# Mixing-layer weights of the first stream: high parts by casting DMA, low parts by an accumulating DMA, loads two units ahead

## The chip, the cores and the metric

The kernel runs on one core of one Trainium2 chip. The metric is device time in microseconds (us). Before the change the median of three runs is 2050.35 us (2050.03 to 2053.55). One profiled execution of the same kernel took 2050.04 us; all rows below come from it.

Engines have short names in the rows: PE is TensorE (PEld its weight loads), DVE is VectorE, ACT is ScalarE, POOL is GpSimd, SP is SyncE. An engine's name with a q behind it (SPq, POOLq) is its instruction queue where it issues a DMA or waits.

## What is computed

One encoder layer on two streams of 512 tokens with 1024 features (a prompt and a sample), each on its own:

```
x = x + 0.5 * swiglu(rms_norm(x, ffn1_norm), ffn1_w_gate, ffn1_w_up, ffn1_w_down)
h = rms_norm(x, mix_norm)
proj = h @ w_in            # q k v | mlstm q k v | 16 gates | o_pre | g_att | g_mlstm
att = gqa_block_attention(rope(rms_norm(aq)), rope(rms_norm(ak)), av)   # 8 heads of 64, 2 kv heads
mem = mlstm_bidirectional(mq, mk, mv, gate_pre, ..., o_pre, ...)        # 4 heads of 128, both directions
merged = sigmoid(g_att) * (att @ w_up_att) + sigmoid(g_mlstm) * (mem @ w_up_mlstm)
x = x + merged @ w_out
x = x + 0.5 * swiglu(rms_norm(x, ffn2_norm), ffn2_w_gate, ffn2_w_up, ffn2_w_down)
```

All inputs and weights are float32 in HBM. Both streams use the same weights.

## The kernel before

**Split arithmetic.** Every large product is made from float32r operands that come in two parts, a high part `hi` (the value rounded to float32r) and a low part `lo` (the value minus `hi`), as three matmuls: hi·hi, hi·lo and lo·hi. So each weight is needed as such a pair. A pair of 1024 columns on 128 partitions, `w`, holds 2 x 512 KB and serves 24 matmuls of 128x512.

**Stages.** The first feed-forward block (helpers at L372 and L630) runs first, then the mixing layer of the prompt, `mix(0)`, then that of the sample, `mix(1)`, then the second feed-forward block. In the trace the mixing layer of the prompt lies between about 640 and 1045 us. Inside it come, in this order: the projections to k, v, gates and q (`tok_proj`, L797); the first mLSTM queries and keys (`mem_qk`); the attention of 8 heads, whose chain of scores (L1083), maximum, exponential (L1088), scaling (L1091, L1093), transposes (L1099), split (L713, L714) and values (L1110) leaves gaps on PE, which are filled with projection matmuls handed out a few at a time (`among`, L817); the mLSTM values (`mem_values`, L797 again); four mLSTM heads (`mem_head`: products L1234, twenty exponentials each at L1248; `mem_out`); eight projections for the merge gate (`mem_gate`, L830) and eight for the mLSTM's way up (`merge_mem`, four weights that each serve two units), one after the other with little else between; and w_out.

**How a weight comes in.** A unit is a pair (load, compute). `go(...)` (L768) calls a unit's load and holds its compute back until the next unit's load has been called. `load_w` (L286) is that load. In `mix(0)` it calls `fetch_w`: SP fetches the raw weight from HBM into a tile `wr` (L271; four buffers). `split_w` then makes the pair in a tile `w` (tag `w8`, four buffers): ACT writes `hi` as a rounded copy (L278), DVE writes `lo` as raw minus `hi` (L279). SP then writes both parts to a scratch area in DRAM, `wpark` (L301), and `mix(1)` reads the pair back from there, with no split of its own. `shifted(-60)` gives ACT's and DVE's part an earlier place in the order.

**Order.** The engines' instruction orders are fixed when the program is built, by a scheduler that goes by these priorities; instructions inside `pin(...)` keep the order in which the code writes them. A DMA waits in its queue's order: what stands behind it on that queue waits too.

**Other names.** `box` tiles (four) hold a broadcast copy of the mLSTM gate sums, `ebuf`, for one head: SP reads them (L1053), and POOL or DVE adds a mask (L1056). The mLSTM's queries and keys of a head (`qk`) lie, for the prompt, in one buffer of tag `w8`; for the sample in two of tag `wr`. `gate_tops` (L983) makes two small transposes (L984, L985) of the gates' running maximum.

Of the kernel before, what the change touches and what calls it, by code (L numbers as in the profile page):

```python
# [9 lines left out]
F32R = mybir.dt.float32r  # L10
# [16 lines left out]
def encoder(ctx, tc, I, outs):  # L27
# [233 lines left out]
    def fetch_w(view, behind=None):  # L261

        views = view if isinstance(view, list) else [view]
        shape = list(views[0].shape)
        shape[2] = sum(v.shape[2] for v in views)
        raw = wpool.tile(shape, F32, tag="wr", bufs=4, name=nm("wr"))
        if behind is not None:
            nc.gpsimd.tensor_copy(raw[:, 0, 0:1], behind)
        c = 0
        for v in views:  # L270
            nc.sync.dma_start(raw[:, :, c:c + v.shape[2]], v)  # L271
            c += v.shape[2]
        return raw
# [9 lines left out]

    parked = {}

    def load_w(view, key):  # L286


        if key in parked:
            d, shape = parked[key]  # L290
            w2 = wpool.tile(shape, F32R, tag="w8", bufs=4, name=nm("w"))
            for i in range(2):
                nc.sync.dma_start(f(w2[:, i]), d[:, i])
            return w2[:, 0], w2[:, 1]
        raw = fetch_w(view)
        with shifted(-WEIGHTS):
            hi, lo = split_w(raw, V_)
        shape = [P, 2] + list(raw.shape[1:])
        parked[key] = d, _ = dpool.tile(shape, F32, name=nm("wpark")), shape
        for i, t in enumerate((hi, lo)):  # L300
            nc.sync.dma_start(d[:, i], f(t))  # L301
        return hi, lo


# [459 lines left out]


    held = []

    def go(*units):  # L768
        for load, comp in units:
            held.append((comp, load()))  # L770
            while len(held) > 1:
                c, w = held.pop(0)
                c(w)

# [29 lines left out]
    def proj(view, key, src, n, done):  # L804

        def comp(w):
            done(proj_w(*w, src, n))

        def steps(w):
            p = []  # L810

            def step(k, i):
                if not p:
                    p.append(MM())
                (wh, wl), (sh, sl) = w, src(k)
                a, b = ((wh, sh), (wh, sl), (wl, sh))[i]
                pin(nc.tensor.matmul(p[0], a[:, k, :], b, start=(k == 0 and i == 0), stop=(k == n - 1 and i == 2)))  # L817
                if k == n - 1 and i == 2:
                    done(p[0])
            return [lambda k=k, i=i: step(k, i) for k in range(n) for i in range(3)]  # L820

        comp.steps = steps
        return (lambda: load_w(view, key)), comp

    def proj_w(wh, wl, src, n, p=None):
        p = p or MM()
# [10 lines left out]
    def mix(s, xh, xl, early=None, extra=None, after=None):  # L837
# [143 lines left out]

        def gate_tops(run, top):
            p = PT()  # L983
            nc.tensor.transpose(p[:, 0:32], run, ident[0:32, 0:32])  # L984
            nc.tensor.transpose(p[:, 32:64], top.to_broadcast([32, P]), ident[0:32, 0:32])  # L985
            V_.tensor_copy(st[:, 0:2], p[:, 0:64].rearrange("p (i d b h) -> p i d b h", i=2, d=2, b=4))


# [12 lines left out]

        def mem_qk(h, j):
            def done(pp):
                if j == 0 and not s:
                    t = wpool.tile([P, 4, S], F32R, tag="w8", bufs=4, name=nm("qk"))
                    qks[h] = [t[:, i] for i in range(4)]
                elif s:
                    t = wpool.tile([P, 2, S], F32R, tag="wr", bufs=4, name=nm("qk"))
                    qks.setdefault(h, []).extend(t[:, i] for i in range(2))
                t = pp  # L1010
                if not s:
                    t = F2()
# [6 lines left out]
        def out_gate(h):  # L1019
# [3 lines left out]
                ogs[h] = og  # L1023
            return win_cols(2320 + h * P, done)

        def q_rope(pr):
            return rope_steps(qraw[:, :, pr * P:(pr + 1) * P], rq[0][:, :, 2 * pr:2 * pr + 2], tabs[0])

# [6 lines left out]
        go(*tok_proj(xh, xl, [(512, 256), (2304, 16)], 2, kv_done, (PS, PS, MM, MM)))  # L1035
        if early:
            early()
        go(*tok_proj(xh, xl, [(0, 512)], 2, q_done, (MM, PO, MM, MM)), mem_qk(0, 0))
        yield None
        tops = gates()  # L1040
        list(q_rope(0))
        with shifted(60):
            k_turn()
            q_turn(0, lambda i: i)
        gate_tops(*tops)
        yield None
        go(mem_qk(0, 1), mem_qk(1, 0), mem_qk(1, 1))

        def mem_rows(h, d):

# [86 lines left out]
                    between.extend(c.steps(w))  # L1137
                between.pop(0)()

        def att_gate(d):  # L1140
            def done(pp):
                gate_of(mg[:, d, :], pp)
            return win_cols(2832 + d * P, done)

        queue.extend(att_gate(d) for d in range(4))
        queue.extend(out_gate(h) for h in range(HM))
        queue.extend(att_gate(d) for d in range(4, 6))
        if not s:
# [8 lines left out]
        for h in range(HA):  # L1157
            nxt = []
            for b in range(4):
                if h in (0, 2, 4) and b == 2:  # L1160
                    q_turn(h // 2 + 1, pin)
                if (h, b) in ((0, 3), (2, 3)):
                    rope = q_rope(h // 2 + 2)
                if h < 4:
                    next(rope, None)
                if h + 1 < HA:
                    nxt.append(score(h + 1, b))
                among(FILLER[0])
# [17 lines left out]
        def up_unit(part, d, src, done, bank=None):  # L1186
            def load():
                if d % 2 == 0:
                    wv = I[("w_up_att", "w_up_mlstm")[part]][0].rearrange("(k p) c -> p k c", p=P)
                    wups[part, d // 2] = load_w(wv[:, :, d * P:(d + 2) * P], ("up", part, d))  # L1190

            def comp(_):
                wu = wups[part, d // 2]
                cl = slice((d % 2) * P, (d % 2 + 1) * P)
                done(proj_w(wu[0][:, :, cl], wu[1][:, :, cl], lambda k: (src[:, k, 0, :], src[:, k, 1, :]), 4,
                            bank and bank()))
            return load, comp
# [100 lines left out]
        for h in range(HM):  # L1298
            Ts = mem_head(h)
            if h == 0:  # L1300
                go(*mem_values())
            queue.append(merge_att(2 * h))
            fill(1)
            mem_out(h, Ts)
            if h + 2 < HM:
                queue.extend([att_gate(h + 6), mem_qk(h + 2, 0), mem_qk(h + 2, 1)])
            queue.append(merge_att(2 * h + 1))
            fill(99)

        mh, ml = A([P, KD, S], F32R, "mh"), A([P, KD, S], F32R, "ml")  # L1310
# [539 lines left out]
```

## Time and profile before

| | |
|---|---|
| median of the runs | 2050.35 us (2050.03 to 2053.55) |
| profiled execution | 2050.04 us |
| its span | 2048.3 us, 1.7 us less than that execution's time |
| PE busy | 2032.9 us, 99% |
| DVE busy | 1564.0 us, 76% |
| ACT busy | 901.6 us, 44% |
| POOL busy | 93.1 us, 5% |
| SP's DMA queue | 450.27 MB, 65.2% of the 16 DMA engines' span |

PE is granted full clock all along (0.999 on average). A group row names line, engine, operation, output<-input, shapes and count, then busy us, mean ns of one, and the idle time before it with what ended that. A DMA row names count, KB each and the median us from issue to landing.

### The profile page before, as it was taken

What the parts mean: (1) busy time and instruction counts of PE and PEld (TensorE: products, weight loads), DVE (VectorE), ACT (ScalarE), POOL (GpSimd) and SP (SyncE); (2) the same over time, 40 slices, a digit from 0 to 9 for tenths busy, and PEclk for the clock granted to TensorE, in tenths of its full rate; (3) what the DMA queues carried; (4) which work ended last, traced back from release to release, by engine and by line L of the source; (5) the groups of instructions that cost most, each with busy time, mean ns of one, the idle gap of its engine ahead of it and who ended that gap; (6) DMA issues with size and microseconds to landing.
All of it is one profiled execution on the core that took longest, in us unless ns stands there. A gap on an engine that the chain in (4) does not pass through costs nothing.

```text
span 2048.3 us, 26765 instructions
## 1 busy us (share of the span) xinstructions
PE 2032.9 (99%) x9317; PEld 1678.7 (82%) x9317; DVE 1564.0 (76%) x2772; ACT 901.6 (44%) x1647; POOL 93.1 (5%) x116
## 2 busy tenths in 40 slices
PE   9999999999999999999999999999999999999998
PEld 7888888888888878888878888888888888888887
DVE  8888888886797888786566746446788988786797
ACT  7644444442234567563324553324444444442224
POOL 0000000001003000100120000001000000000001
PEclk9999999999999999999999999999999999999999
DMA  9656566799766853868684345677655655599753
GB/s 318 199 168 224 176 201 195 243 344 351 262 224 225 289 165 126 274 227 286 202 316 157 113 141 188 217 260 253 195 185 186 198 173 185 199 344 344 273 200 119
DMA packets 311014, 457.96 MB, mean 224 GB/s; under 512 B 20232, under 2 KB 182112, under 8 KB 309600
## 3 DMA queue, kind: packets, MB, share of 16 engines
q1 hardware_dynamic: 308800, 450.27, 65.2%
q0 software_dynamic: 1920, 5.72, 0.8%
q8 instruction: 73, 1.20, 0.2%
q14 instruction: 61, 0.50, 0.1%
q10 hardware_dynamic: 160, 0.27, 0.0%
HBM read 288.25 MB, written 167.94 MB: 223 GB/s over the span
## 4 chain that ended last, share of the span: by engine, by line
PE 94%; DVE 3%; ACT 1%; DMA 1%; issue 0%; SPq 0%; ACTq 0%; DVEq 0%
PE mm L830 15%; PE pst L372 12%; PE pso L372 12%; PE mm L372 10%; PE mm L630 8%; PE pss L372 6%; PE mm L817 5%; PE pss L630 4%; PE pst L630 4%; PE mm L797 4%; PE pso L630 3%; PE pso L1110 1%; PE pss L1083 1%; PE pst L1099 1%; PE pso L1284 1%; PE pss L1234 1%
## 5 line engine op out<-in xcount | busy, mean ns | idle before, releaser
L372 PE MATMUL pst<-xc,w 128*128 128x512 f32 x1056 | 253.6, 389 | 0.0
L372 PEld LDWEIGHTS pst<-xc,w 128*128 128x128 f32 x1056 | 198.2, 188 | 41.1
L372 PE MATMUL mm<-xc,w 128*128 128x512 f32 x972 | 229.6, 390 | 0.5 <-ACT f L380 0.5
L372 PEld LDWEIGHTS mm<-xc,w 128*128 128x128 f32 x972 | 182.0, 188 | 38.4 <-ACT f L380 0.9
L630 PE MATMUL mm<-rt,w 128*128 128x512 f32 x765 | 178.7, 389 | 0.0
L830 PE MATMUL mm<-xh,w 128*128 128x512 f32 x560 | 176.2, 392 | 0.0
L630 PEld LDWEIGHTS mm<-rt,w 128*128 128x128 f32 x765 | 143.5, 188 | 29.8
L330 ACT ACTIVATE w<-t 128x512 fp32r<-128x512 f32 x176 | 106.5, 627 | 135.7 <-issue 63.1
L331 DVE TENSOR_TENSOR w<-t,w 128x512 fp32r<-128x512 f32 x176 | 117.7, 687 | 41.5 <-ACT w L330 39.9
L372 PE MATMUL pss<-xc,w 128*128 128x512 f32 x528 | 126.8, 389 | 0.0
L372 PE MATMUL pso<-xc,w 128*128 128x512 f32 x528 | 126.8, 389 | 0.0
L372 PE MATMUL pso<-xc,f 128*128 128x512 f32 x528 | 126.8, 389 | 0.0
L830 PEld LDWEIGHTS mm<-xh,w 128*128 128x128 f32 x560 | 104.9, 188 | 21.5
L372 PEld LDWEIGHTS pso<-xc,f 128*128 128x128 f32 x528 | 99.1, 188 | 20.6
L372 PEld LDWEIGHTS pss<-xc,w 128*128 128x128 f32 x528 | 99.1, 188 | 20.6
L372 PEld LDWEIGHTS pso<-xc,w 128*128 128x128 f32 x528 | 99.1, 188 | 20.6
L817 PE MATMUL mm<-xh,w 128*128 128x512 f32 x336 | 114.6, 401 | 0.0
L830 PE MATMUL mm<-xl,w 128*128 128x512 f32 x280 | 109.7, 392 | 0.0
L713 ACT ACTIVATE w<-wr 128x512 fp32r<-128x512 f32 x72 | 45.1, 632 | 137.2 <-PE pso L630 71.8
L713 ACT ACTIVATE w<-t 128x512 fp32r<-128x512 f32 x82 | 51.8, 632 | 107.4 <-PE pst L630 62.4
L630 PE MATMUL pss<-rt,w 128*128 128x512 f32 x396 | 93.7, 389 | 0.0
L630 PE MATMUL pst<-rt,w 128*128 128x512 f32 x396 | 93.7, 389 | 0.0
(440 smaller groups left out, 4005.6 us busy)
## 6 DMA issues: line engine op xcount, KB each, us to landing
rt<-rbuf SPq DMA_DIRECT2D x154, 512.0 KB, 5.4
wpark<-w SPq DMA_DIRECT2D x104, 512.0 KB, 3.5
w<-wpark SPq DMA_DIRECT2D x104, 512.0 KB, 4.9
wr<-in_ffn_w_gate_dram SPq DMA_DIRECT2D x62, 512.0 KB, 5.4
rbuf<-tab SPq DMA_DIRECT2D x102, 256.0 KB, 3.9
wr<-in_ffn_w_up_dram SPq DMA_DIRECT2D x44, 512.0 KB, 4.5
rbuf<-f SPq DMA_DIRECT2D x72, 256.0 KB, 4.1
wr<-in_w_in_dram SPq DMA_DIRECT2D x36, 512.0 KB, 6.4
```

The costliest lines, as they stand in the source:

```text
L330: pin(nc.scalar.activation(t[:, 0], src, AF.Copy))
L331: pin(V_.tensor_tensor(t[:, 1], src, f(t[:, 0]), op=ALU.subtract))
L372: nc.tensor.matmul(p, a[:, k, :], xt[:, b, k, :], start=(first and k == 0 and i == 0), stop=(k == HK_ - 1 and i == 2), skip_group_check=True)
L630: nc.tensor.matmul(p, u[:, a, d * P:(d + 1) * P], r[:, b, ts], start=(first and q == 0 and k == 0), stop=(q == len(us) - 1 and k == 2), sk ...
L713: nc.scalar.activation(hi, src, AF.Copy)
L797: nc.tensor.matmul(p[b][:, :N], a[:, k, bs], w_[:, kl, :], start=(k == 0 and i == 0), stop=(k == KD - 1 and i == 2))
L817: pin(nc.tensor.matmul(p[0], a[:, k, :], b, start=(k == 0 and i == 0), stop=(k == n - 1 and i == 2)))
L830: nc.tensor.matmul(p, a[:, k, :], b, start=(k == 0 and i == 0), stop=(k == n - 1 and i == 2))
L1083: pin(nc.tensor.matmul(p, qT[:, h, b * P:(b + 1) * P], kv[:, hk * 2 + j, :], start=(j == 0), stop=(j == 1)))
L1099: pin(nc.tensor.transpose(p[:, b * P:(b + 1) * P], Ps[b][:, kb * P:(kb + 1) * P], ident))
L1110: pin(nc.tensor.matmul(pos[h], Vst[:, kb, h // 4, :], w, start=(kb == 0 and i == 0), stop=(kb == 3 and i == 1)))
L1234: nc.tensor.matmul(p, qk[a][:, isl], qk[b], start=(n == 0), stop=(n == 2))
```

## The change

`load_w` gets a flag `cast`. It is set for the 28 units that `win_cols` makes (8 `mem_qk`, 4 `out_gate`, 8 `att_gate`, 8 `mem_gate`) and for the 8 loads of `w_up_att` and `w_up_mlstm`: 36 weights of 512 KB. For these, in `mix(0)`, POOL's queue issues a DMA from HBM straight into `hi`, which rounds to float32r on the way; ACT writes `lo = -hi`; POOL's queue issues a second DMA from HBM that adds the raw weight onto `lo`. SP's raw fetch, the `wr` tile and DVE's subtraction are gone for them; the two writes to `wpark` stay. The weights of `tok_proj` (keys, values, gates, queries, mLSTM values) and of w_out come in as before.

`go` holds two units instead of one. The two transposes of `gate_tops` are pinned behind the second score of the second attention head. `mem_qk` units and the first `att_gate` are called earlier, the prompt's `qk` tiles lie in two `wr` buffers per head as the sample's do, and `merge_att(1)` is queued beside `merge_att(0)`. This applies to both streams, except where `not s` is written; the casting path acts in `mix(0)` alone, since `mix(1)` finds its pairs parked.

```diff
-    def load_w(view, key):
+    def load_w(view, key, cast=False):
...
-        raw = fetch_w(view)
-        with shifted(-WEIGHTS):
-            hi, lo = split_w(raw, V_)
-        shape = [P, 2] + list(raw.shape[1:])
+        if cast:
+            hi, lo = cast_w(view)
+        else:
+            raw = fetch_w(view)
+            with shifted(-WEIGHTS):
+                hi, lo = split_w(raw, V_)
+        shape = [P, 2] + list(hi.shape[1:])
         parked[key] = d, _ = dpool.tile(shape, F32, name=nm("wpark")), shape
         for i, t in enumerate((hi, lo)):
             nc.sync.dma_start(d[:, i], f(t))
+        return hi, lo
+
+    def cast_w(view):
+
+        w2 = wpool.tile([P, 2] + list(view.shape[1:]), F32R, tag="w8", bufs=4, name=nm("w"))
+        hi, lo = w2[:, 0], w2[:, 1]
+        nc.gpsimd.dma_start(hi, view)
+        with shifted(-WEIGHTS):
+            nc.scalar.activation(lo, f(hi), AF.Copy, scale=-1.0)
+            nc.gpsimd.dma_start(lo, view, accum_op=ALU.add)
         return hi, lo
...
     held = []
+    AHEAD = 2
...
-            while len(held) > 1:
+            while len(held) > AHEAD:
...
-        return (lambda: load_w(view, key)), comp
+        return (lambda: load_w(view, key, key[0] == "in")), comp
...
-            nc.tensor.transpose(p[:, 0:32], run, ident[0:32, 0:32])
-            nc.tensor.transpose(p[:, 32:64], top.to_broadcast([32, P]), ident[0:32, 0:32])
+            pin(nc.tensor.transpose(p[:, 0:32], run, ident[0:32, 0:32]))
+            pin(nc.tensor.transpose(p[:, 32:64], top.to_broadcast([32, P]), ident[0:32, 0:32]))
...
-                if j == 0 and not s:
-                    t = wpool.tile([P, 4, S], F32R, tag="w8", bufs=4, name=nm("qk"))
-                    qks[h] = [t[:, i] for i in range(4)]
-                elif s:
-                    t = wpool.tile([P, 2, S], F32R, tag="wr", bufs=4, name=nm("qk"))
-                    qks.setdefault(h, []).extend(t[:, i] for i in range(2))
+                t = wpool.tile([P, 2, S], F32R, tag="wr", bufs=4, name=nm("qk"))
+                qks.setdefault(h, []).extend(t[:, i] for i in range(2))
...
-        go(*tok_proj(xh, xl, [(0, 512)], 2, q_done, (MM, PO, MM, MM)), mem_qk(0, 0))
+        go(*tok_proj(xh, xl, [(0, 512)], 2, q_done, (MM, PO, MM, MM)), mem_qk(0, 0), mem_qk(0, 1))
...
-        gate_tops(*tops)
         yield None
-        go(mem_qk(0, 1), mem_qk(1, 0), mem_qk(1, 1))
+        go(mem_qk(1, 0), mem_qk(1, 1), att_gate(0))
...
-        queue.extend(att_gate(d) for d in range(4))
+        queue.extend(att_gate(d) for d in range(1, 4))
...
+                if (h, b) == (0, 1):
+                    gate_tops(*tops)
...
-                    wups[part, d // 2] = load_w(wv[:, :, d * P:(d + 2) * P], ("up", part, d))
+                    wups[part, d // 2] = load_w(wv[:, :, d * P:(d + 2) * P], ("up", part, d), True)
...
-            fill(1)
+            if h == 0:
+                queue.append(merge_att(1))
+            fill(2)
...
-            queue.append(merge_att(2 * h + 1))
+            if h:
+                queue.append(merge_att(2 * h + 1))
```

Three places in the instruction orders show what this moves. The number at the end of a name is that of one buffer use.

**POOL in the stretch of mLSTM heads and merge gates.** Before the change POOL's whole order between the gates' copies (L952, L954) and the low parts of the merge (L714) is one row:

```order
L952 COPY Is_430_5645<-gt_363_5277 128x16
L954 COPY Is_430_5645<-gt_363_5277 128x4 x4
L1056 TENSOR_TENSOR box_360_5274<-box_360_5274,tab_301_4214 128x512 x6
L714 TENSOR_TENSOR ml_911_8043<-mg_365_5279,mh_910_8042 128x512 x6
L952 COPY Fs_1050_8991<-gt_985_8558 128x16
```

Now (L311 the casting DMA, L314 the accumulating one, same queue; the eight `mem_gate` weights begin with w_891, the four of `w_up_mlstm` with w_921):

```order
L311 DMA w_894_8031<-in_w_in_dram 128x8x128
L314 DMA w_894_8031<-in_w_in_dram 128x8x128
L311 DMA w_897_8052<-in_w_in_dram 128x8x128
L314 DMA w_897_8052<-in_w_in_dram 128x8x128
L311 DMA w_901_8087<-in_w_in_dram 128x8x128
L314 DMA w_901_8087<-in_w_in_dram 128x8x128
L311 DMA w_905_8122<-in_w_in_dram 128x8x128
L314 DMA w_905_8122<-in_w_in_dram 128x8x128
L311 DMA w_909_8157<-in_w_in_dram 128x8x128
L311 DMA w_913_8192<-in_w_in_dram 128x8x128
L314 DMA w_909_8157<-in_w_in_dram 128x8x128
L314 DMA w_913_8192<-in_w_in_dram 128x8x128
```

Each weight has two issues on one queue, and but for a few pairs the next weight's cast stands behind this weight's accumulate.

**SP around the end of the attention.** `wr` tiles here are the raw mLSTM values' weights (128x2x512), `box` the gate sums of a head. Before:

```order
L271 DMA wr_642_6651<-in_w_in_dram 128x8x128
L301 DMA wpark_568_6326<-w_567_6323 128x1024 x2
L271 DMA wr_733_7038<-in_w_in_dram 128x2x512
L301 DMA wpark_594_6432<-w_593_6429 128x1024 x2
L271 DMA wr_736_7046<-in_w_in_dram 128x2x512
L301 DMA wpark_618_6544<-w_617_6541 128x1024 x2
L271 DMA wr_743_7082<-in_w_in_dram 128x2x512
```

Now:

```order
L304 DMA wpark_586_6429<-w_585_6425 128x1024 x2
L304 DMA wpark_609_6540<-w_608_6536 128x1024 x2
L1067 DMA box_360_5274<-ebuf_367_5281 128x4x128
L271 DMA wr_721_7026<-in_w_in_dram 128x2x512
L271 DMA wr_724_7034<-in_w_in_dram 128x2x512
L1067 DMA box_360_5274<-ebuf_367_5281 128x4x128
L304 DMA wpark_723_7031<-w_722_7028 128x1024 x2
```

The first two of these fetches stood among the attention's traffic; now they stand behind a read into `box` for the second mLSTM head.

**ACT at the same place.** L1248 (now L1259) are the first mLSTM head's twenty exponentials, L1261 (now L1272) the scaling after them, L278 the high part of a raw weight. Before:

```order
L278 ACTIVATE w_737_7048<-wr_736_7046 128x1024
L1088 ACTIVATE t2_693_6860,asm_692_6858<-pss_691_6855,asm_692_6858 128x512
L713 ACTIVATE t2_695_6869<-pst_694_6864 128x512
L1088 ACTIVATE t2_699_6880,asm_698_6878<-pss_697_6875,asm_698_6878 128x512
L713 ACTIVATE t2_701_6889<-pst_700_6884 128x512
L1091 ACTIVATE t2_699_6880<-t2_699_6880,asm_698_6878 128x512
L713 ACTIVATE t2_704_6900<-pst_703_6895 128x512
L1121 ACTIVATE f2_707_6907<-pso_690_6852 64x512
L713 ACTIVATE t2_709_6915<-pst_708_6910 128x512
L713 ACTIVATE t2_713_6927<-pst_712_6922 128x512
L713 ACTIVATE t2_716_6938<-pst_715_6933 128x512
L1248 ACTIVATE t2_722_6976<-box_360_5274,st_368_5282 128x128
```

Now:

```order
L1259 ACTIVATE t2_720_7009<-box_360_5274,st_368_5282 128x128
L1272 ACTIVATE t2_710_6964<-t2_710_6964,dn_708_6959 128x128
L1272 ACTIVATE t2_713_6977<-t2_713_6977,dn_708_6959 128x256
L1272 ACTIVATE t2_716_6990<-t2_716_6990,dn_708_6959 128x384
L278 ACTIVATE w_722_7028<-wr_721_7026 128x1024
L1272 ACTIVATE t2_719_7003<-t2_719_7003,dn_708_6959 128x512
L278 ACTIVATE w_725_7036<-wr_724_7034 128x1024
```

The first two weights of the mLSTM values were split during the attention; now their split stands behind the first head's exponentials.

More of the change, by code (lines that the diff above doesn't have):

```diff
@@ L1024, in out_gate, with att_gate, done @@
             return win_cols(2320 + h * P, done)
+        def att_gate(d):
+            def done(pp):
+                gate_of(mg[:, d, :], pp)
+            return win_cols(2832 + d * P, done)
         def q_rope(pr):
@@ L1138, in among @@
                 between.pop(0)()
[L1140 to L1143, printed above, removed]
-        queue.extend(att_gate(d) for d in range(4))
+        queue.extend(att_gate(d) for d in range(1, 4))
         queue.extend(out_gate(h) for h in range(HM))
```

## The prediction

> **What bounds the kernel now.** First the head of the page, then the chain that ended last.
>
> ```profile
> span 2048.3 us, 26765 instructions
> PE 2032.9 (99%) x9317; PEld 1678.7 (82%) x9317; DVE 1564.0 (76%) x2772; ACT 901.6 (44%) x1647; POOL 93.1 (5%) x116
> PE 94%; DVE 3%; ACT 1%; DMA 1%; issue 0%; SPq 0%; ACTq 0%; DVEq 0%
> ```
>
> PE is busy for all but 15 us of the span. The change takes no matmul away, so it can gain only what PE now waits, and can lose without such a limit. The waits of PE between 640 and 1060 us, the whole mixing layer of the prompt:
>
> ```profile
> PE pst L984 <- DVE kv L931: 1.5, 1, 1.5
> PE pss L797 <- DVE t L1215: 0.8, 1, 0.8
> PE pst L1099 <- ACT t L1091: 0.7, 1, 0.7
> PE pst L1099 <- DVE t L1093: 0.4, 1, 0.4
> PE pst L1099 <- DVE t L714: 0.3, 1, 0.3
> PE pst L1099 <- DVE qT L1033: 0.3, 1, 0.3
> ```
>
> They sum to 4.0 us; none is a wait for a weight. Weights now always come in time. How much time they have shows in three stretches (columns: PE busy with its count, PEld, DVE, ACT, POOL, clock, DMA share, GB/s):
>
> ```profile
> 664.00:700.00 36.00, 35.90 (x169) 29.18 (x169) 25.77 (x55) 18.27 (x26) 0.00 (x0) 1.00 0.94 310
> 700.00:803.00 103.00, 101.15 (x500) 82.31 (x499) 90.76 (x185) 70.02 (x138) 0.00 (x0) 1.00 0.51 170
> 700.00:803.00 103.00, 66.14 (x240) 43.37 (x240) 1.00 0.51 170
> 925.00:982.00 57.00, 57.00 (x253) 46.99 (x252) 39.91 (x60) 20.20 (x30) 6.79 (x5) 1.00 0.83 279
> ```
>
> The third row is the second one for L817 alone. A weight serves 24 matmuls. In the attention 240 of L817 are 10 weights in 103 us, 10.3 us each. In the merge stretch 57.00 / 253 is 0.2253 us a matmul, so PE takes a weight in 24 x 0.2253 = 5.41 us. There a new supply path decides.
>
> **What is removed.** DVE's subtraction, 36 times, and SP's fetches:
>
> ```profile
> L279 DVE TENSOR_TENSOR w<-wr,w 128x1024 fp32r<-128x1024 f32 (+1 forms) x56 | 70.3, 1258 | 25.6 <-ACT w L278 21.3 <-DMA f<-xbuf 3.2 <-DMA wr<-in_w_in_dram 0.9
> L278 ACT ACTIVATE w<-wr 128x1024 fp32r<-128x1024 f32 x38 | 39.6, 1054 | 43.7 <-issue 18.0 <-PE mm L830 8.2 <-PE pss L1234 7.6
> ```
>
> 36 x 1.26 = 45 us of DVE go, off PE's path but for the waits listed. If all DVE- and ACT-made waits went, L984's too (its transposes are moved), that is 4.0 us. A little more may hide in the spacing of the attention's matmuls, 401 ns against 389 where nothing interrupts:
>
> ```profile
> L817 PE MATMUL mm<-xh,w 128*128 128x512 f32 x336 | 114.6, 401 | 0.0
> L630 PE MATMUL mm<-rt,w 128*128 128x512 f32 x765 | 178.7, 389 | 0.0
> ```
>
> 240 x 0.011 = 2.6 us at most. After 1060 us both kernels read parked pairs, and between 1060 and 1400 us PE's list of waits is one row, word for word the fifth above, so two units ahead gain at most 0.3. Gains lie between 0 and 6.9; I take 4, the waits that have a row. ACT's negation has the size of its old copy, 1.05 us, so ACT's work is unchanged.
>
> **What is added: a queue that takes turns.** For a weight POOL issues a cast (L311), ACT negates, POOL issues the accumulate (L314), and mostly the next cast stands behind that. While the accumulate waits for ACT, and ACT for the cast's landing, the next weight's transfer can't start; SP's fetches now have no such coupling and run a few weights ahead. Rows for the prices:
>
> ```profile
> L745 POOL DMA_DIRECT2D f<-in_c_rope_dram x1 | 0.9, 918 | 0.0
> L1324 POOL DMA_DIRECT2D x2buf<-f x16 | 8.9, 556 | 381.8 <-DVE f L1323 376.9 <-DVE cs L967 5.0
> wr<-in_w_in_dram SPq DMA_DIRECT2D x11, 512.0 KB, 4.7
> wr<-in_w_in_dram SPq DMA_DIRECT2D x6, 512.0 KB, 6.5
> wr<-in_w_up_mlstm_dram SPq DMA_DIRECT2D x4, 512.0 KB, 5.5
> w<-wpark SPq DMA_DIRECT2D x104, 512.0 KB, 4.9
> wpark<-w SPq DMA_DIRECT2D x104, 512.0 KB, 3.5
> out_dram<-t SPq DMA_DIRECT2D x8, 256.0 KB, 2.2
> GB/s 318 199 168 224 176 201 195 243 344 351 262 224 225 289 165 126 274 227 286 202 316 157 113 141 188 217 260 253 195 185 186 198 173 185 199 344 344 273 200 119
> ```
>
> Issue: L745 has 1024 runs, as a weight of 128x8x128 has, and took 0.92 us (128 runs: 0.56); I take 0.92. Landing of a cast: no casting or accumulating DMA is in the trace. A plain fetch of 512 KB landed in 4.7 us in the attention's window (700 to 830 us, first of the rows) and 5.5 to 6.5 in the merge stretch (890 to 960). Low end: the quickest 256 KB, 2.2, plus 256 KB more at 351 GB/s, 0.75: 3.0 us. High end 6.5. I take 5.2, between the quiet fetch and the up-projections' fetch. Landing of an accumulate: it must also read its target. At least as the cast; at most the quiet fetch and a full read of the tile as long as its park, 4.7 + 3.5 = 8.2. I take 5.7, near the plain fetches, since reading and writing can overlap. Behind one another on a queue: 512 KB at 351 GB/s is 1.5 us at least; I take 2.0 since the parks share the engines.
>
> One turn, from one accumulate's issue to the next: the next cast is issued 0.92 later and lands at 0.92 + 5.2 = 6.1, but not before the accumulate's data plus 2.0, 5.7 + 2.0 = 7.7; then ACT's 1.05 with 0.1 each for two semaphores. 7.7 + 1.25 = 8.95 us. This is under the attention's 10.3 us, so the attention hides it, and 3.54 us over the merge stretch's 5.41.
>
> A rule speaks against the change on top. DVE's scaling in the attention works from SBUF to SBUF:
>
> ```profile
> L1093 DVE TENSOR_SCALAR t<-t,asm 128x512 f32<-128x512 f32 x16 | 7.7, 484 | 0.3
> ```
>
> The Trainium skill, SBUF — State Buffer, its box on the "DVE blocks DMA" trap, says that while DVE runs an operation in a two-port mode, GpSimd can't write descriptors, so its DMAs start late. If L1093 is such an operation, an issue could be late by up to 0.48 us; that lies in the attention's spare 1.35 us a turn, so the sum would be the same, and no run so far shows it.
>
> The sum, place by place.
>
> *Start-up.* The first seven cast weights are used one behind the other at about PE's 36 us for 169 matmuls (7 x 24 = 168), so the seventh is needed about 37 us after the first. The queue gives five turns and one pair (two casts together, 2.0 apart): 5 x 8.95 + 2.0 = 46.8. The first is about 4.4 us early (a cast of 5.2, ACT, an accumulate of 5.7 after the gates' copies). Loss 46.8 - 37 - 4.4 = 5.
>
> *End of the attention.* Now PE fills the last head's gaps with the mLSTM values' projection:
>
> ```profile
> 812.93 0.60 ACT L713 ACTIVATE t<-pst 128x512 fp32r<-128x512 f32 x1 [0.30 <-PE pst L1099]
> 813.43 1.56 ACT L1248 ACTIVATE t<-box,st 128x128 f32<-128x128 f32 x5
> 806.83 0.43 SPq L271 DMA_DIRECT2D wr<-in_w_in_dram  x1
> 840.83 5.96 ACT L1248 ACTIVATE t<-box,st 128x128 f32<-128x128 f32 x20
> 803.00:824.90 21.90, 14.23 (x56) 10.55 (x57) 1.00 0.43 151
> ```
>
> The last row is L797 alone. After the change its first fetch stands on SP behind a read into `box`, and its `wr` buffer is freed by the first head's products; these wait for PSUM that the exponentials and DVE free, so I put the fetch at the fifteenth of twenty exponentials: 15 x 0.30 = 4.5 us after 813.4. Then 0.43 issue, 5.5 landing, 1.05 ACT, 0.1: 825. Up to there PE did 56 matmuls of L797, 56 x 0.2253 = 12.6 us, for which it now has nothing. Without them the last head's chain ends 2 to 3 us sooner. Loss 10. If the fetch gets its buffer and queue place in time, nothing: that is the other end.
>
> *Heads, 820 to 925 us.* Casts come in clumps of three weights that PE takes in 5.4 us each. POOL's queue also has mask additions (1.53 us each), and the negation can stand behind one head's exponentials, 5.96 us:
>
> ```profile
> L1056 POOL TENSOR_TENSOR box<-box,tab 128x512 f32<-128x512 f32 x6 | 9.2, 1526 | 218.4 <-DMA wpark<-w 161.2 <-DMA box<-ebuf 49.2 <-ACT mg L861 8.0
> ```
>
> One clump overruns its reserve by two turns, 2 x 3.54 = 7. Nothing if the reserve holds; 14 if two do.
>
> *Merge stretch.* Twelve weights at 5.41 us. The first is ready about 5.5 us early: its buffer is free three weights ahead, 16.2 us, of which casting, negating and accumulating take 5.2 + 1.25 + 5.7 = 12.2, with 1.5 us of slower need ahead of it. Of the eleven after it nine take a turn and two come as the second of a pair, 2.0 behind the first: 9 x 3.54 - 2 x 3.41 = 25.0, less 5.5 is 19.5. As the need of raw data doubles, the floor by bytes is 4 x 0.524 MB at 351 GB/s (cast, accumulate, two parks), 6.0 us a weight: 12 x 0.6 = 7 even with an ideal queue.
>
> Sum 5 + 10 + 7 + 19.5 = 41.5, and 37.5 with the gain of 4. 2048.3 + 37.5 + 1.7 outside the span = 2087.5, so **2087 us**; the profiled execution is 0.3 us under the median of the runs, so nothing is to be added.
>
> **Rivals.**
>
> *The queue keeps up.* If cast and accumulate land in 3.0 us and follow each other in 1.5, a turn is 3.0 + 1.5 + 1.25 = 5.75 us. The merge stretch then loses 12 x 0.34 = 4 less 5.5 in reserve, nothing; start-up and heads nothing. With the fetch of the values in time too it leaves the gain of 4.0 to 6.9 from 2050.0: 2043 to 2046, faster. For: a POOL queue that does nothing else; against: no 512 KB fetch in these windows landed under 4.7 in the median.
>
> The Trainium skill, DMA: Bandwidth & Descriptors, in its section on the anatomy of a DMA from GpSimd, fits such a DMA as 2.0 us plus its bytes over 436 GB/s; for 512 KB that is an estimate of 3.2 us, which would make this rival true. The trace's only repeated DMA from POOL speaks against it, since by that fit 256 KB would be 2.6 us:
>
> ```profile
> x2buf<-f POOLq DMA_DIRECT2D x16, 256.0 KB, 4.6
> ```
>
> *The accumulate is slow.* At 8.2 us a turn is 8.2 + 2.0 + 1.25 = 11.45, above the attention's 10.3 as well: 1.15 x 10 = 11 more there, 2.5 x 9 = 22 more in the merge stretch, 2.5 x 5 = 12 at the start, some 15 in the heads. 2087 + 60 = 2147. It decides from an accumulate of 7.0 us on (turn 10.3).
>
> *Only the attention's end counts.* Quick DMAs as in the first rival, but the late fetch: 10 less 4.0 to 6.9, 2053 to 2056.
>
> **How the numbers follow.** Forecast 0.53 (its own range 2066 to 2112); queue keeps up 0.19; only the attention's end 0.12; slow accumulate 0.16. The range 2043 to 2135 leaves out most of the slow accumulate and little else. A measurement of this kernel can tell about 0.2%, 4 us, from no change: faster needs under 2046. Faster 0.17, all but a little of the first rival; same 0.09, the rest of it and the lower half of the third; slower 0.74, the others.
>
> **What would show it.** Each step is right if PE's list of waits has L830 and L817 behind POOL's accumulate, twelve times some 3 us between 950 and 1020 us; if L314's issues on POOL lie about 9 us apart there and 10 in the attention; if casts land in 5 and accumulates in 5 to 6 us; and if PE has a gap of some 10 us before its first L811. It is wrong if POOL's issues follow PE at 5.4 us (first rival), if POOL's turns exceed 10 us already in the attention (slow accumulate), or if the gap before L811 is missing.

## The result: 2168.88 us, and the profile after

The changed kernel takes 2168.88 us in the median (2167.0 to 2171.86, 4 runs) against 2050.64 us (2050.03 to 2053.55, 4 runs): slower by a factor of 1.0574, 95% interval 1.0561 to 1.0587, some 118 us. The forecast was 2087, with a range up to 2135. The direction was right, the size a third of what came.

The head of the page of the kernel after, and the chain that ended last:

```profile
span 2167.0 us, 26814 instructions
PE 2071.4 (96%) x9317; PEld 1698.1 (78%) x9317; DVE 1526.8 (70%) x2736; ACT 901.8 (42%) x1647; POOL 177.4 (8%) x188
PE 79%; issue 8%; DMA 6%; DVE 3%; ACT 2%; POOL 2%; SPq 0%; POOLq 0%; ACTq 0%; DVEq 0%
```

PE has the same 9317 matmuls. It is idle for 95.6 us of the span instead of 15.4, and *busy* for 38.5 us longer. DVE lost 37 us of work (45 were forecast), and the kernel is slower all the same.

PE's waits in the kernel after (what waited <- what ended it: total, times, longest):

```profile
PE pss L1097 <- ACT t L1102: 11.9, 2, 9.8
PE mm L844 <- DMA w<-in_w_in_dram: 10.6, 4, 3.9
PE pss L844 <- DMA w<-in_w_up_mlstm_dram: 10.4, 2, 6.3
PE pso L1295 <- ACT t L726: 10.2, 3, 4.7
PE pss L1245 <- DVE t L1261: 7.1, 5, 2.9
```

None of these stood in the list before. Only the second and third are waits for a weight by name. The first and fourth are attention scores and mLSTM values that wait for ACT.

Where the time goes can be read by comparing both kernels at the same amount of PE's work. For each matmul I took the distance from its start to the next one's; what exceeds the distance at full clock (0.227 us for 512 columns) is lost. The lost time up to a point, less what the kernel before had lost at that point, in us:

| up to | end of first projections | middle of attention | late attention | first mLSTM head | start of merge stretch | end of merge stretch | end |
|---|---|---|---|---|---|---|---|
| after | 1 | 42 | 43 | 54 | 84 | 117 | 118 |

So the start-up and the first half of the attention cost 41 us, some 12 and some 29 (predicted: 5 and nothing), the second half nothing, the end of the attention 11 (predicted 10), the heads 30 (predicted 7), the merge stretch 33 (predicted 19.5).

How POOL's queue runs, in the first half of the attention, where POOL's casts and accumulates and SP's writes to `wpark` are the only transfers:

```profile
733.78 1.54 POOL L314 DMA_DIRECT2D w<-in_w_in_dram  x1 [7.58 <-ACT w L313]
734.66 1.68 POOL L311 DMA_DIRECT2D w<-in_w_in_dram  x1
743.72 1.55 POOL L314 DMA_DIRECT2D w<-in_w_in_dram  x1 [7.38 <-ACT w L313]
744.61 1.57 POOL L311 DMA_DIRECT2D w<-in_w_in_dram  x1
753.21 1.55 POOL L314 DMA_DIRECT2D w<-in_w_in_dram  x1 [7.03 <-ACT w L313]
754.09 1.58 POOL L311 DMA_DIRECT2D w<-in_w_in_dram  x1
```

The predicted alternation is there: accumulate (L314), next cast (L311) 0.9 us behind it, then 7 to 8 us of waiting for ACT's negation. From accumulate to accumulate it is 743.72 - 733.78 = 9.94 and 753.21 - 743.72 = 9.49 us; the five turns from 714 to 764 us took 9.5 to 10.6, 9.9 in the mean. I had put 8.95. An accumulate landed in 6.4 us (I had put 5.7), with hardly any spread for those issued from 723 to 764 us, and the cast issued behind it landed 1.7 to 2.6 us later than it (I had put 2.0).

What the prediction missed is what ACT does meanwhile (start, duration, instruction, in brackets the idle time before):

```profile
722.17 1.06 ACT L313 ACTIVATE w<-w 128x1024 fp32r<-128x1024 f32 x1 [3.90 <-DMA w<-in_w_in_dram]
723.14 0.61 ACT L726 ACTIVATE qk<-f 128x512 fp32r<-128x512 f32 x1
732.34 1.06 ACT L313 ACTIVATE w<-w 128x1024 fp32r<-128x1024 f32 x1 [8.59 <-DMA w<-in_w_in_dram]
733.30 0.61 ACT L726 ACTIVATE qk<-f 128x512 fp32r<-128x512 f32 x1
733.94 0.69 ACT L1102 ACTIVATE t<-pss,asm 128x512 f32<-128x512 f32 x1
```

ACT does its work in order. The negation L313 stands ahead of the first attention exponential L1102 and waits 8.59 us for its cast. The exponential, which needs nothing from that weight, waits with it. Until 728.7 us it could not have run anyway, since its maximum on DVE (L1100) ended only then; for the 5.2 us from there to its start the negation holds it, and a short split behind the negation. DVE was late because of ACT too. It had stood for 9.35 us until ACT's L944, and L944 stood behind the negation before, which had waited 11.45 us for its cast:

```profile
712.75 1.06 ACT L313 ACTIVATE w<-w 128x1024 fp32r<-128x1024 f32 x1 [11.45 <-DMA w<-in_w_in_dram]
714.46 0.68 DVE L945 TENSOR_TENSOR kv<-pst,kv 64x512 fp32r<-64x512 f32 x1 [9.35 <-ACT kv L944]
728.05 0.68 DVE L1100 TENSOR_REDUCE asm<-pss 128x1 f32<-128x512 f32 x1
```

And PE at the time of that exponential:

```profile
724.31 0.39 PE L831 MATMUL mm<-xl,w 128*128 128x512 f32 x1
724.54 0.39 PE L831 MATMUL mm<-xh,w 128*128 128x512 f32 x1
734.77 1.22 PE L1097 MATMUL pss<-kv,qT 128*128 128x512 f32 x2 [9.85 <-ACT t L1102]
735.79 0.63 PE L831 MATMUL mm<-xh,w 128*128 128x512 f32 x1
736.22 0.63 PE L831 MATMUL mm<-xl,w 128*128 128x512 f32 x1
...
740.39 0.39 PE L831 MATMUL mm<-xh,w 128*128 128x512 f32 x1
740.62 0.39 PE L831 MATMUL mm<-xl,w 128*128 128x512 f32 x1
740.85 0.62 PE L831 MATMUL mm<-xh,w 128*128 128x512 f32 x2
```

PE waits 9.85 us for the exponential to free PSUM. Then the matmuls that follow start 736.22 - 735.79 = 0.43 us apart, until about 740 us, when they are back at 0.23. The windows of the kernel after show the reason (columns as before; after POOL comes the granted clock):

```profile
712.00:724.00 12.00, 10.71 (x48) 8.54 (x47) 8.82 (x15) 6.13 (x9) 2.70 (x3) 1.00 1.03 252
724.00:736.00 12.00, 2.15 (x8) 1.46 (x7) 6.93 (x15) 2.35 (x4) 4.42 (x4) 0.75 0.86 183
736.00:748.00 12.00, 8.94 (x32) 6.62 (x31) 5.57 (x12) 4.41 (x9) 2.80 (x3) 0.82 1.01 197
748.00:760.00 12.00, 8.00 (x39) 5.68 (x40) 6.76 (x23) 5.08 (x10) 2.46 (x2) 1.00 1.16 226
```

In the mean of these windows the granted clock falls to 0.75 and 0.82 around the stall and is 1.00 again afterwards. Between 630 and 1130 us the trace has 60 gaps between matmuls of more than 0.25 us beyond the normal distance, 96.8 us in all (before: 9 gaps, 6.0 us), and besides these 103 matmuls that start 0.2 us late, 20.5 us in all (before: none). So of the 118 us about 91 are waiting and 20 are half-speed matmuls behind the waits; the rest is small.

### The profile page after: what moved, and what is told of

It reads as the page before. It is cut to its first block, busy times and chain, and to the rows that moved or that the text cites. A ratio compares the mean times of both kernels' runs of the same rounds, so it can differ in the third digit from the quotient of the medians.

```text
span 2167.0 us, 26814 instructions
## 1 busy us (share of the span) xinstructions
PE 2071.4 (96%) x9317; PEld 1698.1 (78%) x9317; DVE 1526.8 (70%) x2736; ACT 901.8 (42%) x1647; POOL 177.4 (8%) x188
## 4 chain that ended last, share of the span: by engine, by line
PE 79%; issue 8%; DMA 6%; DVE 3%; ACT 2%; POOL 2%; SPq 0%; POOLq 0%; ACTq 0%; DVEq 0%
PE pso L385 11%; PE pst L385 11%; PE mm L844 10%; PE mm L385 10%; PE mm L643 8%; PE pss L385 6%; PE pst L643 4%; PE pss L643 4%; PE mm L831 3%; DMA w<-in_w_in_dram 3%; PE pso L643 3%; PE mm L811 2%; DMA box<-ebuf 1%; PE pso L1124 1%; PE pst L1113 1%
## 5 line engine op out<-in xcount | busy, mean ns | idle before, releaser
L844 PE MATMUL mm<-xh,w 128*128 128x512 f32 x560 | 185.8, 407 | 14.4 <-DMA w<-in_w_in_dram 10.6
L344 DVE TENSOR_TENSOR w<-t,w 128x512 fp32r<-128x512 f32 x176 | 117.6, 686 | 41.7 <-ACT w L343 40.1
L844 PEld LDWEIGHTS mm<-xh,w 128*128 128x128 f32 x560 | 109.6, 197 | 39.4 <-DMA w<-in_w_in_dram 12.3
L831 PE MATMUL mm<-xh,w 128*128 128x512 f32 x336 | 116.1, 406 | 1.3 <-DMA w<-in_w_in_dram 1.3
L313 ACT ACTIVATE w<-w 128x1024 fp32r<-128x1024 f32 x36 | 38.1, 1059 | 183.6 <-issue 82.8
```

Source lines behind the costliest of these rows:

```text
L313: nc.scalar.activation(lo, f(hi), AF.Copy, scale=-1.0)
L344: pin(V_.tensor_tensor(t[:, 1], src, f(t[:, 0]), op=ALU.subtract))
L844: nc.tensor.matmul(p, a[:, k, :], b, start=(k == 0 and i == 0), stop=(k == n - 1 and i == 2))
```

## The experiments

Twelve kernels. Each was timed beside the kernel before on its chip; the kernel before took 2050.3 to 2053.2 us in the medians of those sets.

**Which part of the change costs?** First with only the order of the change, and then with only the new way to load.

Kernel old_load, from the changed kernel (its `qk` tiles must go back to tag `w8`, since four `wr` buffers held by `qk` would leave none for the raw fetches):

```diff
-        if cast:
+        if False:
             hi, lo = cast_w(view)
...
-    AHEAD = 2
+    AHEAD = 1
...
-                t = wpool.tile([P, 2, S], F32R, tag="wr", bufs=4, name=nm("qk"))
-                qks.setdefault(h, []).extend(t[:, i] for i in range(2))
+                if j == 0 and not s:
+                    t = wpool.tile([P, 4, S], F32R, tag="w8", bufs=4, name=nm("qk"))
+                    qks[h] = [t[:, i] for i in range(4)]
...
```

> All 36 weights come in as before (SP fetch, ACT high part, DVE low part, qk of the prompt in w8, one unit ahead); the rest of the change's order stays (gate_tops later, mem_qk and att_gate earlier, merge_att(1) beside merge_att(0)). Theory of turns (cast, ACT, accumulate, next cast on one POOL queue): nearly all of the loss is gone, 2043 to 2060 us, at the lower end if the 1.7 us wait at gate_tops goes, at the upper if the values' weights still come late. Rival that the order is the cause: 2100 us or more.

Measured: 2059.51 us (2057.57 to 2063.5), ratio 1.0048, interval 1.0034 to 1.0063. The order costs some 9 us by itself; it isn't the cause of the 118. In this kernel's trace the end of the attention costs 0.1 us more than before, not 11: with `qk` back in `w8` the values' weights come in time. Most of its loss lies after 1045 us, in the sample's mixing layer.

Kernel old_order is the kernel before with `cast_w` added and called for the same 36 weights; nothing else.

> The kernel before with nothing but the new way to load the 36 weights: one unit ahead, old order, qk in w8. Theory of turns: still slow, 2120 to 2200 us, and no faster than the change, since one unit less of lead is left to hide a turn of 9 to 10 us. Rival that two ahead or the order makes the loss: within 10 us of 2050.

Measured: 2166.66 us (2164.07 to 2169.25), ratio 1.0565. The same loss without any of the change's order, and with one unit ahead instead of two. So the loading path is the cause. By the count of lost time above, this kernel loses nothing at the end of the attention (its `qk` lies in `w8`) and some 13 us more elsewhere. So the change's order with two units ahead does hide some of the loss, and its late values' weights give that back.

Kernel tops_only is the kernel before with `gate_tops` pinned behind the second score of the second head:

> The kernel before with only gate_tops moved behind the second score of the second attention head and pinned, as in the change. PE's 1.5 us wait at L984 should go: 2047.5 to 2050 us against 2050.3. Rival that the moved work is late elsewhere (its DVE copy among the attention's): 2050 to 2055 us.

Measured: 2052.16 us against 2051.31, ratio 1.0003, interval 0.9994 to 1.0012. No difference, although the wait at L984 is gone from PE's list of waits. The one gain that the prediction had a row for can't be measured.

**Is it ACT, or the queue?** Kernel dve_neg moves the negation from ACT to DVE:

```diff
-            nc.scalar.activation(lo, f(hi), AF.Copy, scale=-1.0)
+            nc.vector.tensor_scalar(lo, f(hi), -1.0, None, op0=ALU.mult)
```

> The change with the negation on DVE instead of ACT. Theory of turns: a turn keeps its two landings and loses at most 0.5 us, so 2140 to 2170 us. Rival that ACT is what stalls, because a negation that waits for its cast's landing holds the attention's exponentials behind it in ACT's order: 30 us or more go, at most 2135 us, and PE's waits for the attention's exponentials (11.9 us) vanish.

Measured: 2172.62 us (2170.12 to 2175.12), 2.6 us above the range of the theory of turns and far from its rival's 2135. But it doesn't clear ACT's part: PE's waits for the attention's exponentials fell from 11.9 to 4.9 us, and its other waits show that DVE now holds up what stands behind the negation.

```profile
PE mm L844 <- DMA w<-in_w_in_dram: 12.9, 4, 5.6
PE pst L985 <- DVE fa L983: 12.4, 1, 12.4
PE pss L844 <- DMA w<-in_w_up_mlstm_dram: 9.2, 2, 5.8
PE pss L1245 <- DVE t L1261: 9.1, 3, 5.8
PE pst L1287 <- DVE t L1273: 7.7, 4, 2.7
```

Kernel pool_neg puts it on POOL (`nc.gpsimd.tensor_scalar`), where it can hold up nothing but its own queue.

> The change with the negation on POOL itself, where it holds only POOL's own queue; ACT and DVE no longer wait for a cast. POOL's turn grows by its slower negation (about 2 us for 1024 columns by its 1.4 us for a 512-column addition), so it is at least 11 us against 9.6. Theory that POOL's turn alone is the price: slower than the change, 2180 us or more. Theory that ACT standing still behind the negation makes a large part: 2165 us or less in spite of the longer turn.

Measured: 2205.73 us (2204.68 to 2206.78). The longest turn gives the slowest kernel, though neither ACT nor DVE waits for a cast now. Here PE waits thirty times for a weight's DMA, ten of them in the attention, where seven are 1.2 to 1.7 us. So a turn alone can make such a loss. But this turn is 11.4 to 11.8 us in the attention, above PE's 10.3 us a weight, and the change's 9.9 is below it. What the change's own turn costs without ACT's waits, this kernel doesn't say.

**Coupling, accumulating, bytes.** A square of four kernels. In kernel decoupled the low part begins as a constant, so that neither ACT nor the accumulate waits for the cast; the low parts come out as the raw weights:

```diff
-            nc.scalar.activation(lo, f(hi), AF.Copy, scale=-1.0)
+            nc.scalar.activation(lo, eps.unsqueeze(2).to_broadcast(list(lo.shape)), AF.Copy, scale=0.0)
```

> The change with the low part begun from a constant (-0 x 1e-6 on ACT) instead of the negated high part, so the computed low parts are the raw weights: same DMAs, same bytes, same ACT time, but neither ACT nor the accumulate waits for the cast. Theory of turns: cast and accumulate then follow each other in about 3.5 us, under PE's 5.4, and what is left is the late values' weights and bytes: 2050 to 2075 us. Rival that bytes or the accumulates themselves set the pace: 2110 us or more.

Measured: 2102.09 us (2101.01 to 2103.17). Between the two: 67 us of the 118 go, 52 stay. The coupling is the larger half, but the queue has a rate of its own. ACT isn't quite free here either: its constant waits for the buffer to come free, 40.1 us in all, and PE once waits 4.5 us for an exponential. This is the kernel's view of the DMAs in the merge stretch, 915 to 1020 us (KB each, median us from issue to landing):

```profile
w<-in_w_in_dram POOLq DMA_DIRECT2D x16, 512.0 KB, 14.8
w<-in_w_up_mlstm_dram POOLq DMA_DIRECT2D x8, 512.0 KB, 17.4
```

A backlog: the accumulates of this stretch landed one after the other from 935.7 to 1017.5 us, eleven steps of 7.4 us in the mean, while PE wants a weight every 5.4.

Kernel two_casts is decoupled with a plain casting DMA as its second one:

```diff
-            nc.gpsimd.dma_start(lo, view, accum_op=ALU.add)
+            nc.gpsimd.dma_start(lo, view)
```

> The decoupled kernel with its second DMA a plain casting one instead of an accumulating one (low parts become the raw weights, as there): same count of DMAs and the same bytes from HBM, but the target isn't read and added to. Theory that the accumulate itself is slow: a weight then takes the queue some 4 us, under PE's 5.4, and the time falls to 2055 to 2075 us. Rival that the doubled raw bytes beside the parks set the rate: 2095 us or more, as decoupled.

Measured: 2073.06 us (2072.62 to 2073.49). With the same bytes from HBM, not adding saves 29 us. Of the 22 us that are left 11 lie at the end of the attention, where the values' weights come late as in the change, and 10 at the end of the merge stretch.

Kernel coupled_casts has ACT's negation of the landed cast again, and the plain second cast:

> The change with its second DMA a plain casting one: same coupling (ACT negates the landed cast, the second DMA waits for ACT, the next cast stands behind), but nothing is read and added (low parts become the raw weights). With the kernels decoupled (2102) and two_casts (2073) this makes a square. If coupling and accumulating add up, 2169 - 29 = 2140 us. If the coupled turn is what decides and a plain second DMA lands 2 us sooner (4.4 against 6.4 us), the turn is 7.6 us and much of the loss goes: 2095 to 2125 us. If only the accumulate mattered: at most 2080 us.

Measured: 2127.41 us (2126.29 to 2128.53), just outside the second of the three. The square, in us over the kernel before in each set's median:

| | second DMA casts | second DMA accumulates |
|---|---|---|
| uncoupled | 22 | 52 |
| coupled | 77 | 118 |

Coupling costs 55 to 66, accumulating 30 to 41; they make each other worse by 11. In the first half of the attention coupled_casts issues its second DMAs 7.8 to 8.1 us apart (716.18, 724.12, 732.03, 739.82, 747.95 us), against 9.5 to 10.6 with the accumulate. Such a turn is far below PE's 10.3 us a weight, and still this half costs some 16 us, with one wait of PE of 6.8 us for an exponential and none for a weight. There it is ACT's standing still that costs, not the queue's pace.

Kernel no_accumulate drops the second DMA from the change; the low parts stay the negated high parts:

> The change without the accumulating DMA: the low parts stay the negated high parts, so the computation is another. Casts on POOL and ACT's negation remain. Both theories: 2050 to 2068 us, some 10 of it from the order (the kernel with the old loads in the new order took 2059.5). If casting itself is slow, or ACT's wait for casts holds up the attention: over 2080 us.

Measured: 2094.84 us (2093.01 to 2096.66), which neither theory had; it is on the side of the rival named last. POOL has only casts, half the DMAs of two_casts, and the kernel is 22 us slower than that one. The difference between them is that ACT waits for each cast's landing (two_casts has a second DMA a weight as well, which can only cost). Its casts were not slow; in its attention, 715 to 800 us:

```profile
w<-in_w_in_dram POOLq DMA_DIRECT2D x6, 512.0 KB, 4.4
```

So ACT's standing still is a price of its own, beside the queue's turn: here PE waits 3.3 us in one piece for the first exponential, DVE's and ACT's chains of the heads are late, and none of PE's waits in the prompt's mixing layer is for one of the 36 weights.

**Can the coupling be loosened in place?** Kernel cast_early keeps the change's DMAs but pins POOL's order so that each cast stands ahead of the accumulate of the weight before it:

```diff
-        nc.gpsimd.dma_start(hi, view)
+        pin = tc.keep_in_program_order
+        pin(nc.gpsimd.dma_start(hi, view))
         with shifted(-WEIGHTS):
             nc.scalar.activation(lo, f(hi), AF.Copy, scale=-1.0)
-            nc.gpsimd.dma_start(lo, view, accum_op=ALU.add)
+
+        def low():
+            pin(nc.gpsimd.dma_start(lo, view, accum_op=ALU.add))
...
+        settle()
+        late.append((lo, low))
```

> The change with POOL's order pinned so that each weight's cast is issued ahead of the accumulate of the weight before it; same DMAs, same numbers. Theory that only the coupling of the two (accumulate waits for ACT, ACT for the cast, the next cast behind) costs: most of the 118 us go, at most 2075 us. Theory that the queue's own rate counts as well (the decoupled kernel still needed some 7.4 us a weight in the merge stretch against PE's 5.4): 2090 to 2115 us, about the decoupled kernel's 2102.

Measured: 2156.95 us (2156.62 to 2157.28). Both expectations missed. The view of POOL's waits names what took the place:

```profile
POOL w L314 <- PE mm L866: 73.4, 13, 12.3
POOL w L319 <- ACT w L316: 48.6, 14, 6.9
```

The first row is a new wait: the cast (here L314) waits 73 us for PE to free one of the four `w8` buffers, and the accumulate of the weight before stands behind it. Of the 36 accumulates (L319) 16 were issued 2 to 15 us after the negation that they need. The second row is what is left of the wait for ACT.

**Does the cast lose lead?** Kernel hi_cast is the kernel before with the high part by a casting DMA, the raw weight by SP and the subtraction by DVE: no accumulate, no ACT.

> The kernel before in its own order, with the high part by a casting DMA on POOL, the raw weight still fetched by SP and the low part subtracted by DVE: no accumulate, no ACT in the chain, 36 x 1.05 us of ACT gone, the raw bytes still read twice. Theory: POOL only issues casts, which land about as an SP fetch does (4.4 us quiet), so the loss is gone: 2046 to 2062 us. If casts on POOL are late as such (their landing or the doubled bytes), 2075 us or more.

Measured: 2098.49 us (2095.76 to 2101.8), ratio 1.0235; the rival's side. A casting DMA writes into the `w8` buffer itself, so it can't start before that buffer is free; SP's raw fetches had four `wr` buffers of their own to run ahead in. POOL's waits of hi_cast:

```profile
POOL w L311 <- PE mm L843: 75.3, 12, 20.6
POOL w L311 <- PE mm L830: 51.4, 5, 13.6
```

Kernel late_fetch measures that lead by itself: the kernel before, its own loads, but each of the 36 fetches held back until its `w8` buffer is free.

```diff
+            w2 = wpool.tile([P, 2] + list(view.shape[1:]), F32R, tag="w8", bufs=4, name=nm("w"))
+            hi, lo = w2[:, 0], w2[:, 1]
+            nc.gpsimd.tensor_copy(hi[:, 0, 0:1], eps)
+            raw = fetch_w(view, f(hi[:, 0, 0:1]))
```

> The kernel before, with its own loads (SP fetch, ACT, DVE) for the 36 weights, but each fetch held back until the weight's buffer in tag w8 is free (two one-element copies on POOL ahead of it), which is when a casting DMA into that buffer can start at the earliest. No cast, no accumulate, no bytes more. Theory that lost lead (raw weights no longer fetched ahead into wr) explains why hi_cast took 2098: 2075 to 2110 us. Rival that casts or doubled bytes made hi_cast's loss: at most 2058 us.

Measured: 2073.18 us (2072.41 to 2073.95), 20 us over the kernel before and just under what the theory had. The lost lead is real. If it weighs the same in hi_cast, it is some 20 of that kernel's 48 us; this share is an estimate, since late_fetch makes ACT wait for the held-back fetches too (32.3 us in all), and hi_cast has no such wait. The other 28 are open. In the crowded stretch from 660 to 720 us hi_cast's casts landed in 8.4 us in the median, but SP's own fetches there took 8.9, against 6.9 in the kernel before: both are late, not the cast as such. Whether the doubled bytes, POOL's queue or the order on DVE makes the loss wasn't tried apart.

## Why the prediction was right in direction and wrong in size

- **PE bounds it, at most 4.0 to 6.9 us to gain, and DVE's relief is worth nothing.** Right as far as the runs tell. DVE's busy time fell by 37 us and no gain shows, though no run takes that relief alone; the wait at L984 was worth nothing measurable (tops_only). Two readings are a little off and change nothing: the spacings of 401 and 389 ns differ by 12 ns, not 11, which makes the upper end 7.2, and one fetch of 512 KB in those windows landed in 4.5 us, under the 4.7 named as the least.
- **The queue takes turns.** Right as a mechanism: pool_neg with the longest turn is slowest, decoupled without coupling gains 67 us. The size was 8.95 us; measured 9.5 to 10.6 in the attention. The accumulate's landing, "I take 5.7", is 6.4 there and 5.6 to 10.8 after 860 us, and from the cast's landing to the accumulate's issue it is 1.4 to 1.7 us, put at 1.25.
- **The step that failed first: "the attention hides it", and with it the start-up's 5 us.** The turn was compared with PE's 10.3 us a weight, as if the queue only had to keep pace. But the turn's waiting sits on ACT as well: the negation waits for its cast in ACT's order, ahead of exponentials, tanhs and splits that have nothing to do with it. The prediction priced "ACT's work is unchanged" by its busy time (901.6 before, 901.8 after: true) and never asked what stands behind the waiting instruction there. That is most of the 9.85 us stall at 724 us, directly and through DVE, and of the 24 us that PE waits in all from 713 to 795 us only 1.3 are for a weight. In the start-up too PE's two long waits, 3.7 and 3.6 us, are named after work of ACT and DVE and not after a weight. no_accumulate shows the price without any turn of accumulates, and coupled_casts shows it in the attention with a turn that is shorter than the forecast one. The first cast was also put at 5.2 and took 9.7 us, in a stretch whose DMA share was 0.94 before the change.
- **End of the attention: 10.** Measured 11, with the reason given: it vanishes when `qk` leaves `wr`, both with the old loads (old_load) and with the new (old_order). The forecast sign did not come, though. PE has no gap of some 10 us before its first L811 but one of 1.6; the loss is spread over the last head's and the first mLSTM head's chains, for which PE had no L797 work to fill in.
- **Heads: 7, merge stretch: 19.5.** Measured 30 and 33. In the merge stretch the terms were mis-sized: by decoupled the queue needs 7.4 us a weight there even without coupling, where I had taken 6.0 as the floor by bytes, and coupled the turns were 9.5 to 13.5 us, but for two pairs. In the heads the mask additions named in the prediction cost not their own 1.5 us but what they wait for: twice POOL stands 9.4 and 10.2 us until `box` has landed, with the next accumulate behind it (at 917.73 and 952.33 us).
- **What no term held: the clock.** About 20 of the 118 us are matmuls at half speed after a stall. A sum that adds up idle time is too small by this when single waits get long.
- **The slow accumulate, given 0.16, at 2147 us and "from 7.0 us on".** Nearest in number, and that was luck: in the attention, where it was said to decide, the accumulate landed in 6.4 us. Two of the five turns there did exceed the 10 us named as its sign, by 0.04 and 0.6, but their mean of 9.9 is below PE's 10.3.

## What to carry to other kernels

When an instruction is given a new wait, list what stands behind it on that engine's own order, not only its busy time: here an ACT copy of unchanged length cost some 22 us by itself (no_accumulate against two_casts), because it waited for a DMA in front of work that others needed. A loader that writes straight into the final buffer gives up the lead that a staging buffer gave, even if it saves an engine's work (20 us in late_fetch, which has one unit ahead; two_casts, with two, loses nothing before the end of the attention). And relief for an engine at 76% that PE hardly waits for buys nothing, while PE at 99% has nothing to spare: 91 us of waiting came with 20 us of half-speed matmuls.

## What the runs showed of the hardware

**PE's clock falls after a wait, in steps of 3.41 us.** In the kernel after, the granted clock between 630 and 1130 us is 0.50 in twelve stretches and 1.00 in the rest. The stretches are 3.41, 6.83 or 10.24 us long, one, two or three times 3.41, and their starts lie on one grid of that step. Matmuls of 512 columns then start 0.43 us apart instead of 0.23. After each of the eleven gaps of 3.5 us or more in PE's matmuls the clock stands at half within 1 us. Below that it goes either way: a gap of 3.44 us at 762 us is followed by no such stretch, one of 1.96 us at 1031 us is, and so is one of 2.54 us in decoupled. The Trainium skill, TensorE: Matmul & The Clock Gate, in its section on HAM oscillation, warns of idle gaps over some 3.4 us; the traces agree about the size, but the limit isn't sharp in them.

**A cast from POOL is quick, an accumulate isn't.** With little beside it, a casting DMA of 512 KB landed in 4.4 us (no_accumulate), no later than SP's plain fetch (4.7 in the kernel before). In the first half of the attention the accumulating one landed in 6.4 us, and the second cast that coupled_casts issues in its place in 4.3 to 4.8. The fit of 2.0 us plus bytes over 436 GB/s (the Trainium skill, DMA: Bandwidth & Descriptors, on the anatomy of a DMA from GpSimd) gives an estimate of 3.2 us: near the cast once its 0.9 us of issue is taken off, not the accumulate. Behind one another in a busy stretch a cast and an accumulate take POOL's queue 7.4 us together (decoupled); with two casts, two_casts was 29 us faster.

**What an issue on POOL takes.** In the kernel after, the issue of a cast took 0.8 to 1.0 us by itself and 1.1 to 1.7 us right behind an accumulate's; the issue of an accumulate took 1.3 to 1.6 us also by itself. In two_casts, where there are only casts, every issue took 0.7 to 1.0 us.
